# Products with zeros at twenty places of TensorE's program where it waits, in a hybrid RWKV-7 and mLSTM layer with a mixture of experts

## The chip, the cores and the metric

One core of a Trainium2 chip runs the whole layer in one launch. The metric is the device time of that launch in microseconds (us): the median of several runs. Engines are named TensorE (PE in the profile, with PEld for its weight loads), VectorE (DVE), ScalarE (ACT), GpSimd (POOL) and SyncE (SP, which here issues DMAs). TensorE multiplies a stationary operand, which is loaded first, with a moving operand of up to 512 columns, and writes into one of eight accumulation banks.

## The reference

The input x is 512 tokens of width 1024; 16 learned tokens are put ahead, so 528 are computed.

```
xn = rmsnorm(h);  proj = xn @ w_in          # r k v (512 each), q k (256 each), v o (512 each), gates
y_a = rwkv7(xn, r, k, v, ...)               # 8 heads of 64, per token:
      Sa = S a_t;  S = S * d_t + Sa b_t' + v_t k_t';  y_t = S r_t
      # the decay d and the rates a come from low-rank products with tanh and sigmoid; then a norm per head and a gate g
y_b = mlstm(q, k, v, o, gates)              # 4 heads, chunks of 64 tokens, matrix memory C, normaliser n, maximum m
h  = h + concat(y_a, y_b) @ w_out
xn = rmsnorm(h)
group = argmax over 4; the best 2 of its 8 experts, gate = pg * pe / sum(pe)
h  = h + sum over the two:  gate * ((silu(xn @ w_gate) * (xn @ w_up)) @ w_down)    # 32 experts, width 512
out = rmsnorm(h)[:, 16:]
```

## The kernel before

The serial recurrences are computed in chunks of 64 tokens. The RWKV heads go in four pairs j = 0..3 (two heads of 64 fill the 128 partitions). For each pair, `decays` (L788) makes decay and rate from 12 products of 64x264 (two times six), `norms` and `heads` the scaled vectors, `products` (L912) in two groups g of 32 products of 64x192 the triangular matrices inside all eight chunks, and at its end `p0`, those of the 16 learned tokens. `valued` (L890) brings v into place with four products into `pvt` and one into `pv0`. `inverse` (L1382) with `interleaved` (L1345) inverts the triangular matrices of all chunks and heads at once: VectorE does 31 serial steps, then TensorE joins the halves with 32x32 products (`pZ`, `pM`). `chain` (L1490) then goes through the chunks -1 to 7 one after the other: `removals` (L1432), `solved` (L1448), `next_state` (L1458), `outputs` (L1472). `gate_a` (L1313) makes the output gate in four accumulation groups of four products (`pgg`). The mLSTM half (`gates` L1133, `states` L1201, `outputs_b` L1259), the output projection with its residual (`mixer` L1866), and the experts follow. The experts run in 16 pairs in the loop at L2058: gate and up products at L2072, down products at L2130, weights fetched by DMA (L1740).

The projections of the input (`projections`, L1018) go in blocks given by the string PLAN (L34): 48 products of 128x264 in fp32r (8 steps k of 6), each block accumulating in two banks, or 24 of 128x512 for an `o` block. They are what TensorE does between the steps of the chain. The first blocks, before anything else can run, are computed in the loop at L632 to L648: for each k = 0..7, ScalarE and VectorE split the k-th slice of the input into a high and a low part, and `proj_k` (L600) multiplies with them.

The order of instructions on TensorE and SyncE is written by a planner, the class `Weave` (L359): each of the functions above is a generator with a rank, added in L1964 to L1983, and the planner goes on with the generator of the lowest rank whose time has come. `need` yields until a planned clock (class `Clock`, L181) says that the operands are written; `bank` yields until a bank is free. Every call through `P` (TensorE) or another engine's wrapper tells this clock what it costs (L300). The order on VectorE, ScalarE and GpSimd is left to the compiler's scheduler, which works with a simulated timeline (L2343). On the chip each engine runs its own program in order and waits at an instruction whose operands or whose bank are not ready.

At the start, nine products with zeros run before the first real one (L615 to L623):

```
    idle_ = A.get([128, 64], name="idle")
    V.memset(idle_, 0.0)
    pi = B.get(1, "idle", rest)
    for i in range(WARM):
        P.matmul(pi, idle_.bitcast(BF16), idle_.bitcast(BF16)[:, None].to_broadcast([128, 4, 128]), start=True, stop=True)
    B.put(pi)
    A.put(idle_)
```

Of the kernel before, what the change touches and what calls it, by code (L numbers as in the profile page):

```python
# [11 lines left out]
BF16 = mybir.dt.bfloat16  # L12
# [18 lines left out]
WARM = 9  # L31
FAR, EDGE = 0, 10
BLOCKS = "projected"
PLAN = "KLMRKRKVRVqRVvVvvqqqveaboooo"  # L34

CV = {}
# [322 lines left out]
class Weave:  # L359
# [4 lines left out]
    def __init__(self, clock, banks):  # L364
        self.clock, self.banks = clock, banks
        self.streams = []
        self.marks = set()
        self.spare = []
        self.n = self.rank = 0

    def add(self, rank, gen):
# [72 lines left out]
def layer(ctx, tc, a, out, dbg=None, stop=None):  # L444
# [169 lines left out]

    idle_ = A.get([128, 64], name="idle")  # L615
    V.memset(idle_, 0.0)
    pi = B.get(1, "idle", rest)
    for i in range(WARM):
        P.matmul(pi, idle_.bitcast(BF16), idle_.bitcast(BF16)[:, None].to_broadcast([128, 4, 128]), start=True, stop=True)
    B.put(pi)  # L620
    A.put(idle_)
    def squares(k):
        sq = A.get([128, L], name="sq") if k else acc  # L623
        if k % 2:
# [8 lines left out]
    for k in range(8):  # L633
        S.activation(xh[k], xT[:, k], AF.Copy, scale=c("nmw", k))
        V.scalar_tensor_tensor(xl[k], xT[:, k], c("nmw", k), xh[k].bitcast(F32), op0=OP.mult, op1=OP.subtract)
        proj_k(pk, kh_, kl_, k)
        if not k:
            first_block(2, 8)
            A.put(kraw)
        if k == 2:  # L640
            k1h, k1l, kput1 = split_block(stream.loaded.pop(0), hi_by=S, lo_by=V)
            for i in range(k):
                proj_k(pk1, k1h, k1l, i)
        if k >= 2:
            proj_k(pk1, k1h, k1l, k)
            squares(k - 2)
    for k in range(6, 8):
        squares(k)  # L648


    W = Weave(clock, B)
# [136 lines left out]
    def decays():  # L788

        yield from until("hwa")  # L790
        for j in range(4):
            if j > 1:
                yield from until(f"P{j - 2}")
            yield from W.units(A, 5)
            res = []
            js = slice(128 * j, 128 * j + 128)
            for i in range(2):
                yield from need(wah, wal, lbh, lbl)
                pg = yield from bank(2, "pg", rest)
                q = PAR[i]  # L800
                for n, (w, x) in enumerate(((lbh, wah), (lbh, wal), (lbl, wah))):
                    for h in range(2):
                        P.matmul(pg[:, h, :264], w[q, js], x[q, h * 264:h * 264 + 264], start=(n == 0),
                                 stop=(n == 2))
                t = A.get([128, L], name="sg" if i == 0 else "al")
                S.activation(halves(t), pg[:, :, :264], AF.Tanh, scale=0.5, bias=dv[:, 16 + 4 * i + j:17 + 4 * i + j])
                B.put(pg)
                G.tensor_scalar(t, t, 0.5, 0.5, op0=OP.mult, op1=OP.add)
                res.append(t)
                yield  # L810
            sg, al = res
            V.tensor_tensor_scan(sg, rst, sg, 0.0, OP.mult, OP.add)
            Dt = A.get([128, 537], name="Dt")
            D65 = Dt[:, 17:].rearrange("p (c t) -> p c t", t=65)
            G.memset(Dt[:, 0:1], 1.0)
            G.memset(D65[:, :, 0:1], 1.0)
            S.activation(Dt[:, 1:17], sg[:, :NM], AF.Exp, scale=-DEC)
            S.activation(D65[:, :, 1:], chunks(sg), AF.Exp, scale=-DEC)
            S.activation(sg, sg, AF.Exp, scale=DEC)
            gcopy(DT[:, j, 0:1], Dt[:, 16:17])  # L820
            gcopy(DT[:, j, 1:9], D65[:, :, 64])
            gates_of[j] = sg, al, Dt, D65
            W.mark(f"D{j}")
        A.put(wah, wal, lbh, lbl, rst)

    def norms():

        for j in range(4):
            yield from until(f"k{j}")
            yield from W.units(A, 1)  # L830
            sq = A.get([128, L], name="sq")
            S.activation(sq, kx[j], AF.Square, scale=c("k_k", j))
            yield from need(sq)
            pn = yield from bank(2, "pn", rest)
            for h in range(2):
                P.matmul(pn[:, h, :264], m("bones"), sq[:, h * 264:h * 264 + 264], start=True, stop=True)
            V.tensor_scalar(halves(sq), pn[:, :, :264], 1e-24, None, op0=OP.max)
            B.put(pn)
            S.activation(sq, sq, AF.Ln)
            S.activation(sq, sq, AF.Exp, scale=-0.5)  # L840
            V.scalar_tensor_tensor(sq, kx[j], c("k_k", j), sq, op0=OP.mult, op1=OP.mult)
            nks[j] = sq
            yield
            W.mark(f"n{j}")
# [45 lines left out]
    def valued(j, v):  # L890


        G.tensor_tensor(BV[:, j], BV[:, j], v[:, NM:], op=OP.mult)
        yield from need(v)
        pvt = yield from bank(1, "pvt", rest)
        for u in range(4):
            P.matmul(pvt[:, 128 * u:128 * u + 128], v[:, NM + 128 * u:NM + 128 * u + 128], cent, start=True, stop=True)
        pv0 = yield from bank(1, "pv0", rest)
        P.matmul(pv0[:NM, 0:128], v[:, :NM], cent, start=True, stop=True)
        for e in range(2):  # L900
            for p in range(2):
                q = PAR[1 - p]
                src = pvt[PAR[e]].rearrange("p (u x) -> p u x", u=4)[:, :, 64 * p:64 * p + 64]
                S.copy(Vs[q, e::2, j], src)
        S.copy(VU0[0:NM, j, 1], pv0[:NM, 64:128])
        S.copy(VU0[64:64 + NM, j, 0], pv0[:NM, 0:64])
        B.put(pvt, pv0)
        A.put(v)
        yield
        W.mark(f"V{j}")  # L910

    def products(j):  # L912

        for g in range(2):
            cs = slice(4 * g, 4 * g + 4)
            yield from need(Bbd, Kbd, MV)
            pB = yield from bank(2, "pAB", rest)
            pK = yield from bank(2, "pAK", rest)
            for i in range(4):
                xs = slice(192 * (i % 2), 192 * (i % 2) + 192)  # L920
                for pt, st, turn in ((pB, Bbd, 0), (pK, Kbd, 1)):
                    for p in range(2):
                        P.matmul(pt[PAR[p ^ turn], i // 2, xs], st[PAR[p], 4 * g + i], MV[PAR[p], 4 * g + i], start=True,
                                 stop=True)
# [22 lines left out]

        yield from need(K0bd, B0bd, mv0)
        p0 = yield from bank(1, "p0", rest)
        P.matmul(p0[:, 0:80], K0bd, mv0, start=True, stop=True)  # L950
        P.matmul(p0[:, 80:160], B0bd, mv0, start=True, stop=True)
        for p in range(2):
# [65 lines left out]
    def projections():  # L1018
# [3 lines left out]
        for i, kind in enumerate(PLAN):  # L1022
# [10 lines left out]
            for k in range(8):  # L1033
                if two:
                    proj_k(pt, hi, lo, k, cols=cols)
                else:
                    proj_k(pt.rearrange("p (a b) -> p a b", a=1), hi, lo, k, ((NM, T),))
                yield
                if k == 1 and i + 1 < len(PLAN):
                    if PLAN[i + 1] == "e":  # L1040
                        yield from until("lora")
                    ready = prepare(PLAN[i + 1])
                if k == 3:
                    stream.load()
# [268 lines left out]
    def gate_a():  # L1313
# [17 lines left out]
        for j in range(4):  # L1331
            js = slice(128 * j, 128 * j + 128)
            pgg = yield from bank(1, "pgg", every)
            for n, (u, v) in enumerate(((wh, xgh), (wh, xgl), (wl, xgh), (ws[0:96], xs[0:96]))):
                P.matmul(pgg, u[:, js], v, start=(n == 0), stop=(n == 3))
            S.activation(Gw[:, j], pgg, AF.Copy, scale=c("lnx_w", j))
            V.scalar_tensor_tensor(BV[:, j], BV[:, j], c("lnx_b", j), pgg, op0=OP.add, op1=OP.mult)
            B.put(pgg)
            yield
        yield from until("columns")  # L1340
        A.put(*held, hg, misc)
        W.mark("Gw")

# [38 lines left out]
    def inverse():  # L1382
# [12 lines left out]
        for uh in range(2):  # L1395
            yield from need(Y2)
            pZ = yield from bank(2, "pZ", rest)
            quarters = [(p, slice(64 * p, 64 * p + 32), slice(64 * p + 32, 64 * p + 64)) for p in range(2)]
            for u in range(16):
                for p, q0, q1 in quarters:  # L1400
# [10 lines left out]
        for uh in range(2):  # L1411
            us = slice(16 * uh, 16 * uh + 16)
            yield from need(Zs[uh], Y1)
            pM = yield from bank(2, "pM", rest)
            for u in range(16):
                for p, q0, q1 in quarters:
                    P.matmul(pM[q0, p, u * 32:u * 32 + 32], Zs[uh][q1, u], Y1[q1, :, 16 * uh + u], start=True,
# [72 lines left out]
    def chain():  # L1490
# [19 lines left out]
        for ch in range(-1, 8):  # L1510
            first = ch < 0
            vs, vu, nxt = (VU0, VU0, VS[0]) if first else (VS[ch % 2], VU[ch % 2], VS[(ch + 1) % 2])
            n = NM if first else 64
            yield from need(vs)
            removals(ch, first, vs, n)
            yield from need(Wt)
            solved(ch, first, vu, n)
            yield from need(vu)
            if ch < 7:
                next_state(ch, first, vu, nxt)  # L1520
                yield
# [825 lines left out]
```

## Time and profile before

| what | value |
|---|---|
| median of 3 runs | 904.93 us (900.92 to 907.99) |
| the profiled execution | 904.07 us |
| its span (first to last instruction on the engines) | 902.3 us |
| mean granted TensorE clock over the span | 0.958 of full speed |
| busy TensorE / VectorE / ScalarE / GpSimd | 826.9 / 434.1 / 264.3 / 203.1 us |

The profiled execution's own time is 1.8 us longer than its span. The busy times overlap. A granted clock of 1.00 is the 2.4 GHz level of TensorE, 0.50 the 1.2 GHz level. Matmuls are pipelined, so a TensorE that is busy all of a stretch is not always at its peak. Most instructions of the front part bear the line L308, since the wrapper that tells the planner issues them; they are told apart by tile, shape and time.

### The profile page before, as it was taken

What the parts mean: (1) busy time and instruction counts of PE and PEld (TensorE: products, weight loads), DVE (VectorE), ACT (ScalarE), POOL (GpSimd) and SP (SyncE); (2) the same over time, 40 slices, a digit from 0 to 9 for tenths busy, and PEclk for the clock granted to TensorE, in tenths of its full rate; (3) what the DMA queues carried; (4) which work ended last, traced back from release to release, by engine and by line L of the source; (5) the groups of instructions that cost most, each with busy time, mean ns of one, the idle gap of its engine ahead of it and who ended that gap; (6) DMA issues with size and microseconds to landing.
All of it is one profiled execution on the core that took longest, in us unless ns stands there. A gap on an engine that the chain in (4) does not pass through costs nothing. (4 is left out here: it accounts for less than half of the span.)

```text
span 902.3 us, 13658 instructions
## 1 busy us (share of the span) xinstructions
PE 826.9 (92%) x5487; PEld 499.0 (55%) x5488; DVE 434.1 (48%) x819; ACT 264.3 (29%) x505; POOL 203.1 (23%) x278
## 2 busy tenths in 40 slices
PE   7989697878899889999999999999999999999994
PEld 5878596777887767888343444433444423332331
DVE  7677757598746639437132333423333323331324
ACT  5755555634345584312110111001110101001102
POOL 5164625365543328220100000000000000000002
PEclk8988889988998899999999999999999999999998
DMA  6210111311300222989999999999999999999982
GB/s 238 71 42 7 47 63 55 83 34 38 102 25 2 74 84 72 386 329 348 376 406 393 419 420 420 420 420 420 420 420 420 420 421 420 420 419 422 421 349 97
DMA packets 45142, 235.60 MB, mean 261 GB/s; under 512 B 9906, under 2 KB 10290, under 8 KB 21008
## 3 DMA queue, kind: packets, MB, share of 16 engines
q1 hardware_dynamic: 42192, 228.58, 63.6%
q0 software_dynamic: 2160, 3.93, 1.1%
q10 hardware_dynamic: 720, 2.15, 0.6%
q8 instruction: 45, 0.74, 0.3%
q14 instruction: 25, 0.20, 0.1%
HBM read 234.38 MB, written 4.19 MB: 264 GB/s over the span
## 5 line engine op out<-in xcount | busy, mean ns | idle before, releaser
L308 PE MATMUL accs<-arS,arR 128*128 128x264 f32 (+2 forms) x1136 | 180.8, 311 | 8.3 <-DVE arS L308 3.5
L308 PEld LDWEIGHTS accs<-arS,arR 128*128 128x128 f32 (+1 forms) x1136 | 160.6, 199 | 22.4 <-issue 5.5
L308 PE MATMUL accs<-arF 64*64 64x192 f32 (+17 forms) x1361 | 112.6, 289 | 29.8 <-DVE arF L308 20.0
L2072 PE MATMUL accs<-arF 128*64 128x512 f32 x568 | 133.2, 599 | 6.2 <-DMA arF<-wgu 6.1
L2000 DVE TENSOR_TENSOR arF<-arF,accs 128x512 f32<-128x512 f32 x124 | 80.8, 683 | 100.4 <-PE accs L1998 98.9
L308 PEld LDWEIGHTS accs<-arF 64*64 64x64 f32 (+6 forms) x1346 | 83.1, 157 | 46.3 <-DVE arF L308 15.9
L308 POOL TENSOR_TENSOR arF<-arF 128x528 f32<-128x528 f32 (+13 forms) x97 | 89.9, 929 | 83.1 <-DVE arF L308 56.6
L1809 POOL DMA_INDIRECT arM<-hd,arF x15 | 15.1, 1008 | 372.8 <-DVE arF L1799 356.1
L308 DVE TENSOR_TENSOR arF<-arF 64x16 f32<-64x16 f32 (+31 forms) x170 | 90.2, 578 | 7.4 <-POOL arF L308 4.7
L2072 PEld LDWEIGHTS accs<-arF 128*64 128x64 f32 x568 | 37.5, 137 | 87.1 <-issue 65.3
L308 ACT ACTIVATE arF<-arF 128x528 f32<-128x528 f32 (+7 forms) x113 | 59.8, 550 | 74.7 <-DVE arF L308 51.5
L2107 ACT ACTIVATE arF<-accs,arF 128x512 f32<-128x512 f32 x16 | 11.0, 687 | 240.1 <-PE accs L2072 240.1
L308 POOL TENSOR_SCALAR arF<-arF 64x256 f32<-64x256 f32 (+9 forms) x101 | 56.9, 565 | 95.3 <-ACT arF L308 43.2
L2140 DVE SCALAR_TENSOR_TENSOR arO<-accs,arF,arO 128x1024 fp32r<-128x1024 f32 x15 | 19.3, 1284 | 103.2 <-ACT arO L2139 103.2
L2130 PE MATMUL accs<-arF 128*64 128x512 f32 x280 | 63.8, 597 | 0.2 <-DMA arF<-wdn 0.2
L1997 PE MATMUL accs<-arO,OHT 128*128 128x512 f32 x124 | 57.5, 464 | 0.0
L308 ACT COPY arF<-accs 64x256 f32<-64x256 f32 (+7 forms) x111 | 39.8, 370 | 53.8 <-PE accs L308 28.2
L308 DVE TENSOR_TENSOR arF<-accs,arF 128x128 f32<-128x128 f32 (+7 forms) x81 | 35.6, 460 | 29.0 <-PE accs L308 21.1
L1998 PE MATMUL accs<-arO,OHT 128*128 128x512 f32 x124 | 49.0, 395 | 0.0
L308 PE MATMUL accs<-arW,arS 128*128 128x512 f32 x192 | 46.7, 398 | 0.0
L1997 PEld LDWEIGHTS accs<-arO,OHT 128*128 128x128 f32 x124 | 23.3, 188 | 40.4 <-issue 38.1
L2139 ACT ACTIVATE arO<-accs,arF 128x1024 fp32r<-128x1024 f32 x15 | 16.7, 1113 | 98.7 <-PE accs L2130 98.7
(142 smaller groups left out, 930.3 us busy)
## 6 DMA issues: line engine op xcount, KB each, us to landing
arF<-wgu SPq DMA_DIRECT2D x71, 1024.0 KB, 19.8
arF<-wdn SPq DMA_DIRECT2D x35, 1024.0 KB, 19.8
arM<-wgu SPq DMA_DIRECT2D x23, 1024.0 KB, 20.0
arH<-wgu SPq DMA_DIRECT2D x17, 1024.0 KB, 19.8
arN<-wgu SPq DMA_DIRECT2D x16, 1024.0 KB, 18.6
arF<-wb SPq DMA_DIRECT2D x23, 512.0 KB, 3.6
arM<-wdn SPq DMA_DIRECT2D x10, 1024.0 KB, 20.5
arN<-wdn SPq DMA_DIRECT2D x8, 1024.0 KB, 20.4
```

Of the source, the lines that this page charges most:

```text
L308: r = f(*args, **kw)
L1809: nc.gpsimd.indirect_dma_start(out=xt[p % 2], out_offset=None, in_=hd, in_offset=bass.IndirectOffsetOnAxis(ap=idx[:, p % 2:p % 2 + 1], axi ...
L1997: P.matmul(pq, lhs, oh[:, hs], start=True, stop=False)
L1998: P.matmul(pq, lhs, ol[:, hs], start=False, stop=True)
L2000: V.tensor_tensor(hv, hv, pq, op=OP.add)
L2072: P.matmul(pgu[64 * e:64 * e + 64, h], x[:, k, 64 * e:64 * e + 64], w[:, D * e + 512 * h:D * e + 512 * h + 512], start=(k == 0), stop=(k = ...
L2107: S.activation(av, pgu[:, 0], AF.Silu, scale=r1_)
L2130: P.matmul(pdn[64 * e:64 * e + 64, h], aT[:, k, 64 * e:64 * e + 64], w[:, D * h + 512 * e:D * h + 512 * e + 512], start=(k == 0), stop=(k ...
L2139: S.activation(oh, pdf, AF.Copy, scale=g1_)
L2140: V.scalar_tensor_tensor(ol, pdf, g1_, oh.bitcast(F32), op0=OP.mult, op1=OP.subtract)
```

## The change

A table `HOLD` gives a number of products for each of twenty places. `keep(place)` issues that many products of the zero tile `idle_`, read as bf16: 128 stationary columns and a moving operand of 4 times 66, that is 264, columns (256 in `solved` of chunk 7). They are issued directly, not through the wrapper, so the planner's clock doesn't see them and the order of the other instructions on TensorE stays as it was. Where `to` names a bank that the next real products overwrite from their start, the zeros are written there first. Where it doesn't, they are added, as zeros, into the open accumulation of the projection block that is half done (`W.open`, which is set after each step k below 7). Places that have no entry issue nothing (`pn`, `pM`, `next` and other indices). The zero tile is kept until the end of `gate_a` and the bank `pi` until the end of the first loop. The counts add up to 255.

```diff
+HOLD = {("decays", 0, 0): 4, ("decays", 0, 1): 4, ("decays", 1, 0): 4, ("products", 0, 0): 19, ("products", 1, 0): 28,
+        ("decays", 3, 0): 11, ("decays", 3, 1): 20, ("p0", 2): 9, ("pvt", 1): 6, ("pv0", 1): 9, ("pvt", 2): 16,
+        ("pvt", 3): 28, ("pZ", 0): 22, ("solved", -1): 13, ("removals", 3): 9, ("solved", 7): 13, ("pgg", 0): 19,
+        ("first", 1): 8, ("first", 2): 8, ("first", 3): 5}
...
+        self.open = None
...
     V.memset(idle_, 0.0)
+    zeros = idle_.bitcast(BF16)
+
+    def keep(*site, to=None):
+
+        t = W.open if to is None else to
+        for _ in range(HOLD.get(site, 0) if t is not None else 0):
+            nc.tensor.matmul(t, zeros[:, :t.shape[0]], zeros[:, None, :t.shape[1] // 4].to_broadcast([128, 4, t.shape[1] // 4]),
+                             start=to is not None, stop=to is not None, skip_group_check=True)
+
     pi = B.get(1, "idle", rest)
...
-    B.put(pi)
-    A.put(idle_)
...
+        if k:
+            keep("first", k, to=pi[:, :264])
         proj_k(pk, kh_, kl_, k)
...
+    B.put(pi)                                    # after the first loop
...
                 pg = yield from bank(2, "pg", rest)
                 q = PAR[i]
+                keep("decays", j, i, to=None if j > 1 else pg[:, 0, :264])
...
+                keep("pn", j, h)
...
         pvt = yield from bank(1, "pvt", rest)
+        keep("pvt", j)
...
         pv0 = yield from bank(1, "pv0", rest)
+        keep("pv0", j)
...
             pB = yield from bank(2, "pAB", rest)
             pK = yield from bank(2, "pAK", rest)
+            keep("products", j, g, to=pB[:, 0, :264])
...
         p0 = yield from bank(1, "p0", rest)
+        keep("p0", j)
...
+                W.open = (pt[:cols, 0, :264] if two else pt[:cols, :264]) if k < 7 else None
                 yield
...
             pgg = yield from bank(1, "pgg", every)
+            keep("pgg", j, to=pgg[:, :264])
...
+        A.put(idle_)                             # end of gate_a
...
             pZ = yield from bank(2, "pZ", rest)
+            keep("pZ", uh)
...
             pM = yield from bank(2, "pM", rest)
+            keep("pM", uh)
...
             yield from need(vs)
+            keep("removals", ch)
             removals(ch, first, vs, n)
             yield from need(Wt)
+            keep("solved", ch, to=uv[:, 0].rearrange("p j x -> p (j x)") if ch > 6 else None)
             solved(ch, first, vu, n)
             yield from need(vu)
+            keep("next", ch)
```

## Rows read from the trace of the kernel before

**Rows 1.** The page: the span, the busy times of the engines with their share and number of instructions, and the granted clock of TensorE in 40 equal slices of the span, in tenths (9 is 90% or more).
```profile
span 902.3 us, 13658 instructions
PE 826.9 (92%) x5487; PEld 499.0 (55%) x5488; DVE 434.1 (48%) x819; ACT 264.3 (29%) x505; POOL 203.1 (23%) x278
PEclk8988889988998899999999999999999999999998
```

**Rows 2.** The view by stretches: begin and end in us from the span's start, length, then busy time and number of instructions of PE, PEld, DVE, ACT and POOL, the granted clock, the mean busy share of the DMA engines, GB/s. Just after the first zero products; from the end of the output gate to the last experts; inside the experts.
```profile
4.20:7.50 3.30, 1.83 (x8) 0.90 (x6) 1.62 (x10) 2.08 (x4) 0.00 (x0) 1.00 0.93 307
338.70:895.00 556.30, 537.60 (x2717) 245.37 (x2715) 202.89 (x411) 80.46 (x147) 51.49 (x58) 1.00 0.94 382
500.00:890.00 390.00, 379.18 (x1848) 144.05 (x1846) 124.75 (x220) 44.27 (x67) 12.99 (x17) 1.00 0.98 405
```

**Rows 3.** The same view, for the eleven stretches in which the granted clock is 0.50.
```profile
7.60:14.40 6.80, 4.22 (x17) 3.92 (x18) 6.77 (x6) 6.25 (x10) 4.31 (x3) 0.50 1.04 411
52.00:58.70 6.70, 6.48 (x29) 6.19 (x29) 4.67 (x6) 4.96 (x11) 6.20 (x8) 0.50 0.00 1
65.70:72.40 6.70, 6.11 (x40) 4.68 (x41) 5.39 (x10) 2.41 (x5) 1.30 (x5) 0.50 0.34 136
93.00:96.30 3.30, 2.68 (x32) 1.97 (x32) 3.30 (x4) 1.88 (x4) 2.74 (x3) 0.50 0.48 153
110.00:120.20 10.20, 6.99 (x27) 5.96 (x26) 8.23 (x11) 1.88 (x4) 4.01 (x6) 0.50 0.14 51
151.00:154.30 3.30, 3.30 (x15) 2.94 (x14) 2.35 (x5) 0.88 (x4) 1.03 (x5) 0.50 0.00 0
192.00:198.70 6.70, 5.51 (x23) 4.88 (x24) 6.63 (x17) 2.22 (x7) 4.21 (x10) 0.50 0.01 2
219.30:226.00 6.70, 6.70 (x135) 6.63 (x131) 2.70 (x3) 5.02 (x4) 5.04 (x4) 0.50 0.02 5
273.90:280.60 6.70, 6.70 (x64) 6.30 (x65) 2.12 (x5) 1.41 (x2) 0.30 (x1) 0.50 0.00 0
308.00:314.70 6.70, 6.51 (x45) 5.72 (x46) 3.72 (x9) 5.63 (x18) 1.44 (x2) 0.50 0.02 4
335.30:338.60 3.30, 3.30 (x9) 2.55 (x8) 1.78 (x3) 1.67 (x4) 1.84 (x1) 0.50 0.00 0
```

**Rows 4.** The timeline of TensorE: start in us, length in us, engine, line, operation, output and operands with their sizes, number of instructions in the row; in brackets the idle time before it and what ended it. Two groups of `products` (74.78 and 93.62) and the two halves of `decays` of pair 3.
```profile
74.78 1.53 PE L308 MATMUL accs<-arF 64*64 64x192 f32 x32
93.62 2.84 PE L308 MATMUL accs<-arF 64*64 64x192 f32 x32 [4.18 <-DVE arF L308]
108.22 0.99 PE L308 MATMUL accs<-arR 64*128 64x264 f32 x6 [1.83 <-ACT arF L308]
113.36 1.69 PE L308 MATMUL accs<-arR 64*128 64x264 f32 x6 [3.21 <-DVE arF L308]
```

**Rows 5.** The timeline of TensorE, same columns: the nine zero products at the start, and a block of the first projections.
```profile
1.02 3.66 PE L308 MATMUL accs<-arF 128*128 128x512 bf16 x9 [1.02 <-DVE arF L308]
29.68 5.64 PE L308 MATMUL accs<-arS,arQ 128*128 128x264 f32 x44 [0.50 <-DVE arQ L308]
```

**Rows 6.** The timeline of TensorE, same columns: `pv0` of pair 1, `removals` of chunk 3, `solved` of chunk 7, the first product of `pgg`.
```profile
150.87 0.57 PE L308 MATMUL accs<-arF 128*16 128x128 f32 x2 [1.42 <-DVE arF L308]
271.37 0.82 PE L308 MATMUL accs<-arF,arE 128*64 128x64 f32 x10 [1.43 <-DVE arF L308]
306.38 0.68 PE L308 MATMUL accs<-arF 64*64 64x64 f32 x16 [2.01 <-DVE arF L308]
334.00 0.49 PE L308 MATMUL accs<-arW 128*128 128x512 f32 x1 [2.92 <-ACT arW L308]
```

**Rows 7.** The timeline of ScalarE, same columns: copies of projections after `decays` of pair 3, and the activations that follow the chain's last chunk.
```profile
120.17 1.94 ACT L308 COPY arF<-accs 64x256 f32<-64x256 f32 x6 [3.45 <-PE accs L308]
315.35 0.34 ACT L308 ACTIVATE arF<-accs 128x4 f32<-128x4 f32 x2 [1.59 <-PE accs L308]
```

**Rows 8.** The view by stretches, columns as in rows 2: the inversion on VectorE, the stretch after the chain's last chunk, and the stretch after `gate_a`.
```profile
177.00:218.80 41.80, 33.10 (x243) 31.40 (x241) 41.08 (x111) 15.72 (x37) 24.60 (x44) 0.92 0.11 39
315.40:330.50 15.10, 15.10 (x82) 11.94 (x81) 4.44 (x10) 14.93 (x28) 2.02 (x2) 1.00 0.25 95
340.00:350.00 10.00, 10.00 (x45) 8.12 (x44) 9.12 (x7) 3.49 (x6) 9.57 (x7) 1.00 0.46 157
```

**Rows 9.** The timeline of TensorE, columns as in rows 4: `decays` of pair 1, the first products of pair 0 (two rows), projections before the inversion's end, `pZ`, and the projections after it.
```profile
52.27 1.69 PE L308 MATMUL accs<-arR 64*128 64x264 f32 x6 [0.22 <-ACT arF L308]
64.33 0.54 PE L308 MATMUL accs<-arF 64*64 64x192 f32 x2 [1.69 <-DVE arF L308]
66.29 3.51 PE L308 MATMUL accs<-arF 64*64 64x192 f32 x28 [1.43 <-DVE arF L308]
213.49 1.98 PE L308 MATMUL accs<-arS,arR 128*128 128x264 f32 x14 [0.73 <-POOL arR L308]
218.87 3.80 PE L308 MATMUL accs<-arF 32*32 32x32 f32 x128 [3.41 <-DVE arF L308]
222.61 4.71 PE L308 MATMUL accs<-arS,arR 128*128 128x264 f32 x24
```

**Rows 10.** The timeline of TensorE's weight loads, same columns: two of the loads of 128 columns in bf16 among the experts.
```profile
602.39 0.10 PEld L1794 LDWEIGHTS <-arF 128*128 128x128 bf16 x1 [0.81 <-issue]
602.43 0.10 PEld L1797 LDWEIGHTS <-arF 128*128 128x128 bf16 x1
```

## The prediction, made before the changed kernel ran

> **What bounds the kernel now.** I read the page's totals first: the span is 902.3 us, TensorE is busy 92% of it, and the line of its clock is at full speed only from the middle on; in the first 15 slices it drops eleven times or so [rows 1]. The profiled execution took 904.07 us, 1.8 more than its span, and 0.86 below the median of the runs shown (904.93). All sums below go against 904.07; the forecast for the median then adds 0.9.
>
> Then I read the views by stretch. From 338.7 us to 895 the clock is 1.00 and TensorE is busy 537.6 of 556.3 us; from 500 to 890 it is busy 379 of 390 us while the DMA engines are at 0.98 and 405 GB/s [rows 2]. Nothing of the change stands there. So this tail keeps its length and moves as a whole by what the front gains or loses. The front is where the change is, and there no engine is full all the time: it is a chain that goes from VectorE, ScalarE and GpSimd to TensorE and back, and each piece has to be judged by the wait that ends last in it.
>
> The third view is the list of stretches with a granted clock of 0.50, the 1.2 GHz level: eleven of them, 67 us together [rows 3]. For each I looked up what TensorE did before (it waited), and in the same stretch which engine was full. That price is visible in equal work: 32 products of 64x192 take 2.84 us in the stretch at 93 us, and 1.53 us at 74.78, where the clock was full [rows 4]. So TensorE's work at the low level costs nearly twice (2.84/1.53 = 1.86; the six 64x264 products give 1.69/0.99 = 1.71), and a stretch that is full of TensorE's work would end 0.41 to 0.46 of its length earlier at the high level.
>
> **What the change adds.** The counts of the twenty places add up to 255 products, nothing is removed, and the order of the real instructions on TensorE and SyncE stays. A product of zeros has 264 columns of bf16. The nearest rows: nine bf16 products of 512 columns at the start take 3.66 us, 0.407 each, so about 0.21 for 264 columns; 44 products of 264 columns in fp32r, at a full clock, take 5.64 us, 0.128 each [rows 5]. The start's nine ran at the pace that is half of what they would at the high level (0.407 for 512 columns against 0.128 for 264 is 1.6 times per column), so 264 bf16 columns lie between 0.105 (half of 0.21) and 0.128 at the high level, and at 0.21 at the low one. I take 0.11 while the clock is high.
>
> At 0.11 each, 28 products are 3.1 us of the 4.18 us wait before the second group of products of head pair 0; 11 and 20 are 1.2 and 2.2 of the 1.83 and 3.21 us before `decays` of pair 3 [rows 4]; 9 are 1.0 of 1.42 (`pv0`); 9 are 1.0 of 1.43 (`removals` of chunk 3); 13 are 1.4 of 2.01 (`solved` of chunk 7); 19 are 2.1 of 2.92 (`pgg`) [rows 6]. The zeros wait for nothing that is late, so they run inside the wait and end 0.3 to 1.1 us ahead of the real work. Their own cost is nothing at this price; the cover is gone at 0.15 us each (4.18/28).
>
> **Where a full clock would pay**, with the stage's own last wait:
> - 93.0 to 96.3: the 32 products themselves, 2.84 to 1.53, with VectorE waiting for their result: 1.3 us.
> - 113.4 to 120.2: TensorE is busy without a gap [rows 3], and ScalarE's copies at 120.17 had waited 3.45 us for it [rows 7]. 6.8 us times 0.41 to 0.46 is 2.8 to 3.1: 3.0.
> - 151.0 to 154.3: full of TensorE's work (3.30 of 3.30); 1.4 to 1.5: 1.5.
> - 273.9 to 280.6: full too (6.70 of 6.70), the chain of chunks, in which the other engines are idle [rows 3]: 3.0.
> - 308.0 to 314.7: TensorE would save 3.0, but ScalarE, in order, had waited only 1.59 us for it before 315.35, and is then busy 14.93 of 15.1 us [rows 7, 8]. What is late next is ScalarE: 1.5.
> - 335.3 to 338.6: TensorE would save 1.4, but from 340 to 350 GpSimd is busy 9.57 and VectorE 9.12 of 10 us [rows 8]. Bounds 0 and 1.2: 0.6.
>
> **Where it would pay nothing.**
> - 7.6 to 14.4: VectorE is busy 6.77 of 6.80 us [rows 3]; the early products follow its splits.
> - 52.0 to 58.7: GpSimd is busy 6.20 of 6.70 us, VectorE follows it, and TensorE waits for VectorE until 64.33 [rows 3, 9]. `decays` of pair 1 gets four zeros ahead of it in the same bank; bounds 0 and 0.5, I charge 0.25.
> - 65.7 to 72.4: bounds 0 and 1.4. TensorE's waits of 1.69 and 1.43 us get 19 zeros, 2.1 us [rows 9]. But if the stretch at 52 is at a full clock, TensorE arrives there some 3 us earlier and waits longer, beyond what the zeros fill. I take 0.
> - 192.0 to 198.7: VectorE inverts the triangular matrices in 31 serial steps, busy 41.08 of 41.80 us from 177 to 218.8 [rows 8]. TensorE there has time. 0.
> - 219.3 to 226.0: 24 projection products at the low level (4.71 us), 14 earlier ones at the high take 1.98, so 24 would be 3.4; bounds 0 and 1.3 [rows 9]. TensorE will reach the wait before 213.49 (0.73 us, for GpSimd) about 3 us earlier, and no zeros stand there; I expect the clock to fall in that longer wait, the 22 zeros then cost 0.21 each, 4.6 us against a wait of 3.41. 0, and down to -1.2.
>
> Sum: 1.3 + 3.0 + 1.5 + 3.0 + 1.5 + 0.6 - 0.25 = 10.65 us. 904.07 - 10.65 = 893.4; on the scale of the median, 894. Upper end of the gain: with 1.4, 1.3, and 0.6 more, and 1.5 more at 308 if ScalarE's order is helped too, some 15 us, 889. A further 4 us if stretches I do not count shorten VectorE's waits: 885.
>
> **The rivals.**
> *A: the falls move.* When TensorE is faster in one stretch, it arrives earlier at its next wait, which is then longer than in the trace the counts can be compared with, and the clock falls there. For it: the wait that ends right at the fall at 52 is of 0.22 us alone [rows 9], and the zeros leave a quarter to a third of each wait open. Against it: the big waits are filled. If only 93, 113 and 151 pay fully (5.8 us) and the rest is lost again: 904.93 - 5.5 = 899.
> *B, slower: the zeros are late.* If a zero product costs 0.21 us, each place on the chain runs over its wait: 28 x 0.21 - 4.18 = 1.7, then 1.0 (20), 1.2 (22), 1.1 (19), 0.7 (13), 0.5 (9), 0.5 (9), 0.5 (11), 0.9 (the first 19): 8.1 us on 150 products, and about 2 on the smaller places. It decides from 0.15 us each. If the clock stays as it is, that is 904.93 + 10 = 915. Against it: at the start TensorE ran nothing but nine zero products, and from 4.2 on its clock was 1.00 [rows 2, 5].
> *C: the loads come in series.* Each zero product loads its 128 columns again. A bf16 load of 128x128 is busy 0.10 us [rows 10]; added to 0.11 that is 0.21 us, now with a full clock: the 10 us of rival B cancel the 10.65 us gained, 904.
>
> On this the Trainium skill ("TensorE: Matmul & The Clock Gate", "LDWEIGHTS (loading the stationary operand)") puts a load in ns at its number of columns over 1.2, 107 ns for 128, and the page's section "The mechanism" lets a load overlap only products in other row groups, which the zeros are not. By that rule the sum would be rival C's. The trace disagrees on the overlap: two such loads of full height start at 602.39 and 602.43, with 0.10 us each, so they are not paid one after the other [rows 10].
>
> *D: it does something else.* The order on VectorE, ScalarE and GpSimd is left to the scheduler, which sees 255 instructions more; 64 words of on-chip memory and one bank are held longer. A changed order costs or brings a few us by chance: 904, 3 either way.
>
> **How the numbers follow.** Forecast 894: 0.53. A, 899: 0.25. B, 915: 0.07. C, 904: 0.05. D, 904: 0.10. One per cent, 9 us, is about what a measurement of this kernel can tell from no change: under 895.9 is faster, over 914 slower. The forecast's own spread (the halves taken at 65, 219, 308, 335) is 887 to 898 and lies mostly under 895.9; nearly all of A and D is within 1%. So faster 0.52, same 0.40, slower 0.08. The range for 8 in 10 takes in the forecast, its upper bounds, A, and most of C and D: 885 to 905.
>
> **What would show it.** Right: granted clock about 1.00 where rows 3 have 0.50, at 93, 113, 151, 274 and 308 above all; the 32 products at 93 in 1.5 us; groups of 28, 20 and 22 bf16 products at 0.11 us each; the inversion by VectorE starting some 5 us earlier, still 41 us long; the tail unchanged in length. New low stretches likely at about 66 and 213. Wrong: zero products at 0.2 us in a full clock (B, C); as many low stretches as before at other places (A); a tail that takes longer, since the front's gain would then be given back at the experts' loads.

## The result: 0.7% slower

The changed kernel took 909.39 us in the median of 14 runs (905.31 to 912.74), the kernel before 902.66 on the same chip (14 runs): ratio 1.0071, 95% interval 1.0054 to 1.0087, some 6.4 us slower by the ratio. The forecast was 894, with 885 to 905 as its range. Ratios below are each against runs of the kernel before on the same chip; the interval stands in brackets.

The page after, answering [rows 1]: the clock is higher (mean 0.976 against 0.958), 255 products more, and the span is 3.6 us longer.
```profile
span 905.9 us, 14165 instructions
PE 843.6 (93%) x5742; PEld 512.4 (57%) x5743; DVE 430.0 (47%) x819; ACT 265.1 (29%) x505; POOL 204.2 (23%) x278
PEclk9998999998899999999999999999999999999997
```

Six stretches of [rows 3] in the changed kernel, among its new low ones, then the tail of [rows 2] (columns as there):
```profile
52.00:58.70 6.70, 6.70 (x57) 6.16 (x56) 5.01 (x7) 5.24 (x11) 6.08 (x7) 1.00 0.02 4
93.00:96.30 3.30, 2.27 (x29) 1.81 (x30) 2.06 (x4) 2.79 (x6) 0.61 (x2) 1.00 0.00 0
110.00:120.20 10.20, 9.23 (x69) 8.00 (x69) 8.93 (x12) 5.83 (x11) 6.52 (x8) 1.00 0.08 9
151.00:154.30 3.30, 3.30 (x30) 3.30 (x29) 3.25 (x7) 1.79 (x2) 0.11 (x1) 1.00 0.01 2
192.00:198.70 6.70, 5.79 (x48) 5.56 (x48) 6.63 (x19) 3.37 (x10) 5.83 (x15) 1.00 0.23 78
210.70:217.50 6.80, 3.33 (x15) 3.23 (x16) 3.83 (x6) 1.33 (x1) 5.29 (x7) 0.50 0.00 1
224.40:227.70 3.30, 3.30 (x17) 3.30 (x17) 0.98 (x2) 0.88 (x2) 0.31 (x1) 0.50 0.64 209
231.20:234.50 3.30, 3.30 (x47) 3.23 (x42) 1.40 (x2) 2.00 (x4) 0.80 (x2) 0.50 0.36 81
275.60:278.90 3.30, 3.30 (x28) 3.16 (x28) 0.72 (x3) 0.36 (x1) 0.00 (x0) 0.50 0.02 5
308.00:314.70 6.70, 6.35 (x86) 5.19 (x85) 4.68 (x11) 5.97 (x18) 1.88 (x2) 1.00 0.23 71
320.00:323.30 3.30, 2.98 (x13) 2.96 (x14) 0.50 (x2) 3.24 (x7) 0.00 (x0) 0.50 0.00 0
391.60:395.00 3.40, 3.40 (x12) 2.90 (x11) 0.00 (x0) 0.00 (x0) 0.00 (x0) 0.50 1.01 422
500.00:890.00 390.00, 380.21 (x1866) 145.05 (x1862) 125.64 (x221) 43.10 (x61) 11.74 (x13) 1.00 0.99 410
```
The zeros do to the clock what was forecast: 52, 93, 110, 151, 192 and 308 stand at 1.00, and the new fall at 210.7 is where it was expected. Up to 890 us eight low stretches are left, 34 us together (two are not shown, at 12.7 and 67.3), where there were eleven and 67 us; those at 231.2, 320.0 and 391.6 were not foreseen.

TensorE's timeline after (columns as in rows 4), from five stretches:
```profile
91.75 2.97 PE L629 MATMUL accs<-arF 128*128 128x264 bf16 x25
95.76 1.53 PE L313 MATMUL accs<-arF 64*64 64x192 f32 x32 [1.03 <-DVE arF L313]
...
110.82 2.42 PE L629 MATMUL accs<-arF 128*128 128x264 bf16 x20
114.21 0.99 PE L313 MATMUL accs<-arR 64*128 64x264 f32 x6 [0.97 <-DVE arF L313]
...
214.16 3.45 PE L313 MATMUL accs<-arS,arR 128*128 128x264 f32 x14 [7.13 <-POOL arR L313]
217.41 2.70 PE L629 MATMUL accs<-arF 128*128 128x264 bf16 x22
220.04 3.17 PE L313 MATMUL accs<-arF 32*32 32x32 f32 x106
...
306.82 1.58 PE L629 MATMUL accs<-arF 128*128 128x256 bf16 x13 [2.16 <-DVE arF L313]
...
320.32 1.33 PE L313 MATMUL accs<-arS,arR 128*128 128x264 f32 x4 [2.51 <-DVE arF L313]
...
329.27 1.89 PE L313 MATMUL accs<-arS,arR 128*128 128x512 f32 x7 [1.42 <-DVE arF L313]
```
Set beside [rows 4, 6, 9], the same instructions show where time came and went. "Ahead" and "behind" below compare the start of the same instruction in two profiled executions, one of each kernel. At 114.21 TensorE is 0.85 us later than before (113.36), and 6 products take 0.99 in place of 1.69; by 194 it is 6 us ahead. VectorE's inversion, too, ends 6 us earlier, at 211.3. Then the lead is lost: 14 projections wait 7.13 us for GpSimd (0.73 before) and begin at 214.16, 0.7 us later than before; `pZ`, 218.87 before, begins at 220.04. `solved` of chunk 7 follows its zeros at 308.33 (306.38 before), and two waits that were not there (2.51 and 1.42 us) bring TensorE 4.6 us behind at 329. By 339 it has 3.0 of these back (1.6 behind), since it has neither the wait of 2.92 us nor the low stretch that the kernel before has there [rows 3, 6]; a wait at 387 that is 0.6 longer and the new fall at 391.6 take 2.2 again.

Why GpSimd was late, in its timeline after:
```profile
210.60 0.95 POOL L313 TENSOR_SCALAR arF<-arF 64x256 f32<-64x256 f32 x2 [5.71 <-DVE arF L313]
211.50 0.30 POOL L313 MEMSET arF<- 128x256 f32 x1
211.77 2.34 POOL L313 TENSOR_TENSOR arR<-arF,arR 128x1024 fp32r<-128x1024 f32 x1
```
The last row is the split of a projection block, for which TensorE waits. Before, it ran straight after the 128x64 row and ahead of the two copies and the memset; now these, which prepare the chain and wait for the inversion's last steps, stand first, and the engine works in order. ScalarE's timeline after shows a change of order too:
```profile
315.51 0.31 ACT L313 ACTIVATE arF<-accs 128x128 f32<-128x128 f32 x1
315.67 0.25 ACT L313 ACTIVATION_READ_ACCUMULATOR arF<-accs 128x1 f32 x1
315.94 1.28 ACT L313 ACT_TABLE_LOAD   x1
317.23 0.69 ACT L313 ACTIVATE arF<-accs,arF 128x512 f32<-128x512 f32 x1
317.82 0.27 ACT L313 ACTIVATE arF<-accs 128x128 f32<-128x128 f32 x1
...
327.05 0.27 ACT L313 ACTIVATE arF<-accs 128x128 f32<-128x128 f32 x1
```
Sums of squares over 128 columns stand between table loads, as before; but the last one now comes at 327.05, behind three table loads, and VectorE's next step waits for it until 327.44. Before, it came at 321.24, ahead of three table loads that now stand before it:
```profile
321.24 0.26 ACT L308 ACTIVATE arF<-accs 128x128 f32<-128x128 f32 x1
321.60 1.28 ACT L308 ACT_TABLE_LOAD   x1
```

### The profile page after: what moved, and what is told of

The parts are those of the page before. It is cut to its first block, busy times and chain, and to the rows that moved or that the text cites. A ratio compares the mean times of both kernels' runs of the same rounds, so it can differ in the third digit from the quotient of the medians.

```text
span 905.9 us, 14165 instructions
## 1 busy us (share of the span) xinstructions
PE 843.6 (93%) x5742; PEld 512.4 (57%) x5743; DVE 430.0 (47%) x819; ACT 265.1 (29%) x505; POOL 204.2 (23%) x278
## 5 line engine op out<-in xcount | busy, mean ns | idle before, releaser
L313 PE MATMUL accs<-arS,arR 128*128 128x264 f32 (+2 forms) x1136 | 178.6, 309 | 17.2 <-POOL arR L313 7.1
L313 PEld LDWEIGHTS accs<-arS,arR 128*128 128x128 f32 (+1 forms) x1136 | 158.6, 196 | 30.2 <-POOL arR L313 7.3
L313 PE MATMUL accs<-arF 64*64 64x192 f32 (+17 forms) x1361 | 105.4, 276 | 14.7 <-DVE arF L313 9.7
L313 PEld LDWEIGHTS accs<-arF 64*64 64x64 f32 (+6 forms) x1346 | 77.1, 146 | 30.0 <-DVE arF L313 9.2
L313 DVE TENSOR_TENSOR arF<-arF 64x16 f32<-64x16 f32 (+31 forms) x170 | 86.6, 556 | 11.7 <-POOL arF L313 4.6
L313 DVE SCALAR_TENSOR_TENSOR arF<-arF 128x528 f32<-128x528 f32 (+5 forms) x50 | 32.8, 663 | 28.7 <-ACT arF L313 27.7
```

The costliest lines, as they stand in the source:

```text
L313: r = f(*args, **kw)
```

## The experiments

The first theory: the scheduler, once it sees the zeros, orders GpSimd, ScalarE and VectorE otherwise, and that costs more than the clock brings. Rivals: the zero tile, held longer, moves the other buffers; or the zeros themselves are late on TensorE.

| run | median us | ratio to before |
|---|---|---|
| changed kernel | 909.4 | 1.0071 [1.0054, 1.0087] |
| e1 held tile, no zeros | 908.2 | 1.0056 [1.0036, 1.0077] |
| e2 split first | 912.3 | 1.0097 [1.0061, 1.0133] |
| e3 no pvt(3) | 909.0 | 1.0064 [1.0038, 1.0089] |
| e4 no solved(7) | 910.0 | 1.0076 [1.0053, 1.0099] |
| e5 own tile, no zeros | 904.2 | 0.9992 [0.9977, 1.0006] |
| e6 own tile, zeros | 914.1 | 1.0112 [1.0088, 1.0135] |
| e7 zeros, order pinned | 898.7 | 0.9939 [0.9919, 0.9959] |
| e8 ten places, pinned | 896.5 | 0.9908 [0.9886, 0.9931] |
| e9 order of e1 alone | 915.2 | 1.0127 [1.0105, 1.0148] |
| e10 order of the changed kernel alone | 922.1 | 1.0203 [1.0178, 1.0228] |
| e11 e7 without solved(7) | 898.1 | 0.9934 [0.9911, 0.9957] |
| e12 three places, pinned | 901.1 | 0.9966 [0.9946, 0.9987] |
| e13 e7, GpSimd's order free | 902.5 | 0.9988 [0.9969, 1.0006] |
| e14 e7, ScalarE's order free | 907.4 | 1.0030 [1.0009, 1.0051] |
| e15 e7, GpSimd's and VectorE's free | 921.4 | 1.0189 [1.0160, 1.0219] |

(e8 leaves out ten of the twenty places and keeps ten, with 143 products; its label and its expectation miscount them.)

**e1**
```diff
-HOLD = {("decays", 0, 0): 4, ...
+HOLD = {}
```


> The changed kernel with an empty table: no zero product is issued, only the zero tile and its bank are held longer. Theory (the order of GpSimd and ScalarE, set by the scheduler once it sees the zeros, costs the time): within 2 us of the kernel before, eleven stretches at a granted clock of 0.50 as there. Rival (the tile held longer moves the other buffers and that alone costs): 5 to 7 us slower than the kernel before.

The rival came true, against the theory: no zero product, the low stretches of before up to 316, and 5 us lost. The built program has the order of before on TensorE and GpSimd, a changed one on VectorE and ScalarE after 300, and one expert weight DMA of SyncE later in its queue. In its profile TensorE is 5.6 us behind at 328, where the last sum of squares comes late as in the changed kernel, but 0.4 behind at 339; a longer wait at 386 (0.6) and a new fall at 390.8 to 394.2 (1.6) make it 2.9 again. So most of what its profile loses in the end (3.4 us of span) is lost there, without any zeros.

**e2**
```diff
+        gate = splits[-2]          # the split of a projection block on GpSimd
+        with tc.issue_after(gate):
             G.memset(Wt, 0.0)
...
+        with tc.issue_after(gate):
             values(0)
```
(and the same around values(1); `splits` lists GpSimd's splits as they are issued)

> The changed kernel with all its zeros and the same order on TensorE and ScalarE; on GpSimd alone the copies and the memset that prepare the chain are ordered behind the split of a projection block. Theory (these copies wait for the end of the inversion and hold up the split, for which TensorE waits 7.13 us): that wait falls under 2 us, the first pZ product comes 4 to 6 us earlier, and the whole is 4 to 5 us faster than the changed kernel, about 905. Rival (the zeros themselves are late on TensorE, the wait is a symptom): the wait is replaced by another one of the same size, 909 as before.

Half a miss. The 7.13 us wait is gone (3.27 us are left at 204), and `pZ` begins at 216.26 instead of 220.04. But TensorE then waits 2.39 us for ScalarE at `solved` of chunk -1, where the changed kernel waits 0.30, and the whole is not faster: of the 3.8 us 1.6 are left there and 0.2 at 300, and at 400, after falls at 353.8 to 357.2 and 391.4 to 398.2, TensorE is 2.1 us behind the changed kernel. The place was mended and the loss moved on.

**e3, e4**
```diff
-        ("pvt", 3): 28,                      # e3
-        ("solved", 7): 13,                   # e4
```


> The changed kernel without the 28 zero products before pvt of pair 3; built so, GpSimd's order around the inversion's end is that of the kernel before. Theory: a low stretch at about 190 comes back, which costs nothing since VectorE's inversion is the bound there, and the 7.13 us wait goes: 3 to 5 us faster than the changed kernel, 904 to 906. Rival (a full clock at that place is worth something): 909 or slower.

> The changed kernel without the 13 zero products before solved of chunk 7. Theory (these zeros are written into the bank that VectorE is still reading, so they start only when the real products could, and with them ScalarE's order after the chain changed): the wait of 2.16 us before a zero product at 304.7 is gone, solved of chunk 7 comes 1.5 to 2 us earlier, the stretch to 330 another 2 us: 2 to 4 us faster, 905 to 907. Rival (they hold the clock for the chain's last stretch): a low stretch comes back at 308 and the time is 909 or more.

Both missed in the total. In e3 the 7 us wait is gone (1.35 us are left), and TensorE is still ahead of before at 232; the waits at 303, 318 and 329 bring it 5.5 us behind (4.6 in the changed kernel). e4 went as its rival said: `solved` of chunk 7 came no earlier (308.74), and the low stretch came back, at 310 to 317. So neither place alone was the cause, and e1 had shown one that has no zeros in it.

**e5, e6**
```diff
-    zeros = idle_.bitcast(BF16)
+    zt = sb.tile([128, 8], F32, name="zt")
+    nc.gpsimd.memset(zt, 0.0)
+    zeros = zt.bitcast(BF16)         # read with a step of 0 as 128 stationary and 264 moving columns
...
+    B.put(pi)                        # both back where they were
+    A.put(idle_)
-            keep("first", k, to=pi[:, :264])
```
(e5 with an empty HOLD, e6 with the rest of it)

> No zero products; the tile for them is eight words outside the memory that the other buffers share, and the first zero tile and its bank go back where the kernel before puts them back. Theory (holding the 64 words and the bank is what cost 5 us in e1, because it moved other buffers and with them the order on ScalarE and VectorE): the program is the kernel before with one memset more, so its time too, within 2 us. Rival (e1 was slow by chance of the build): 907 or more.

> The zeros of all places but the three of the first loop (234 products), from the tile of e5; the order on VectorE, ScalarE and GpSimd is left to the scheduler. Theory (two costs, the held tile and the orders that the zeros bring about): the part of the held tile is gone, 5 us less than the changed kernel, about 904; the 7 us wait before 214 and late weights or statistics remain where the order differs. Rival (only the held tile costs): all gains of the clock show, 894 to 898.

e5 is the kernel before, in its order on every engine and in its time: what e1 lost came with the held tile. e6 missed on the worse side: without the held tile, but with the orders that 234 zeros bring about, 914.

**e7, e8**
```diff
+    for e, runs in ORDER.items():    # V, S, G: the order in which the kernel before has its instructions
+        ins, line = LOG[e], [t for a0, a1 in runs for t in range(a0, a1)]
+        for i, j in zip(line, line[1:]):
+            tc.add_manual_dep(ins[j], ins[i].name, mybir.DependencyInfo(mybir.DependencyClass.NoSync, mybir.DependencyReason.DATA), reason="order")
```


> As e6, with the order of every instruction on VectorE, ScalarE and GpSimd up to the experts pinned to that of the kernel before; TensorE and SyncE have theirs already. Theory (the zeros do to the clock what the prediction said, and the orders gave it back): few low stretches, TensorE 6 us ahead at 211 and after it, 894 to 898. Rival (zeros on the path cost what the clock gives): 902 to 906.

> As e7, without the zeros at decays of pairs 0 and 1, pvt of pairs 2 and 3, pZ and solved of chunk 7: eleven places, 143 products, those in whose stretch TensorE sets the end or whose zeros wait for no reader of a bank. Theory (these other places cost or bring nothing): as fast as e7 or 1 to 3 us faster, since the 2 to 3 us lost before 67 and the 2 us at solved of chunk 7 are gone: 892 to 897. Rival (low stretches come back at 52, 192 and 219 and count): 2 to 4 us slower than e7.

The decisive pair. e7 has e6's zeros, memory and TensorE program, and only the order on three engines is another: 898.7 in place of 914.1. In the traces e7 has, leaving out the zeros, the order of e5 instruction by instruction, and e5 takes the time of the kernel before; so the order that is pinned brings nothing by itself. e8 has the lowest median: 0.92% under the kernel before, 8.3 us (6.2 to 10.3), though its six runs overlap with those of e7. Both beat both kernels.

**e9, e10** (the program of e5, ORDER taken from e1 and from the changed kernel)

> No zero products and no held tile: the program of e5, with VectorE, ScalarE and GpSimd pinned to the order that they have in e1. Theory (the held tile costs through the order alone): 4 to 6 us slower than the kernel before, 908, with ScalarE's reductions after 315 split by an activation of 512 columns as in e1. Rival (the moved buffers, or the one moved DMA on SyncE, cost in e1): as the kernel before.

> No zero products and no held tile: the program of e5, with VectorE, ScalarE and GpSimd pinned to the order of the changed kernel. Theory (orders cost what the clock brought): the changed kernel without its gains, 914 to 919, with a wait of TensorE for the weights' split before 214. Rival (that order is good only or bad only together with the zeros): 902 to 908.

The orders alone, without a zero or a moved buffer, cost 11.5 and 18.4 us (1.27 and 2.03% of 904). Both lost more than expected (908; 914 to 919). e9 lost more than e1, which has the same order on VectorE, ScalarE and GpSimd: in e9 ScalarE, in order, waits for a weight that had come in time in e1, and so it does in e10 (first e9, then e10):
```profile
318.67 0.62 ACT L316 CAST arW<-arF 128x512 fp32r<-128x512 f32 x1 [5.58 <-DMA arF<-wo]
```
```profile
325.65 0.62 ACT L316 CAST arW<-arF 128x512 fp32r<-128x512 f32 x1 [9.00 <-DMA arF<-wo]
```
In the changed kernel no wait of ScalarE for these weights is longer than 1.1 us. TensorE loses 10.0 us in e9 and 10.7 in e10 between the instructions that the kernel before has at 312 and at 325; e1 and the changed kernel lose 4.8 and 4.3 there. So 11.5 and 18.4 are not what these orders cost in the kernels that they come from; e10 does show the wait for the split (6.21 us before 218.04).

**e11, e12** (pinned; HOLD without solved(7); HOLD with products(1,0), decays(3,0), decays(3,1) alone)

> As e7, without the 13 zero products before solved of chunk 7, which waited 2.09 us for the bank that VectorE was reading and ran behind that wait. Theory (those zeros alone cost 1.5 to 2.3 us there): 896 to 897, solved of chunk 7 at 301.2 to 301.5 instead of 303.4. Rival (without them a low stretch at 308 takes back as much): 898 to 899.

> Order pinned to that of the kernel before; zeros at three places alone: products of pair 1 (28), decays of pair 3 (11 and 20). By the terms of the prediction these bring 1.3 and 3.0 us: 4 us faster than the kernel before, 900, with TensorE 4 us ahead from 121 on. Rival (the gain is given back at the inversion, where VectorE sets the pace, or at the next unfilled wait): 903 to 905.

e11: the theory of those thirteen zeros fell. They do run behind the bank's reader, but without them the clock is at 0.50 from 303 to 310, and the time is the same. e12: 3.1 us (1.2 to 4.9) where 4.3 were expected. In its profile TensorE is 2.2 us behind before 93 and 2.3 ahead at 121, so that the two places bring 4.4.

**e13, e14, e15** (e7 with some engines' ORDER taken from e6)

> As e7 (zeros, pinned order), but GpSimd has the order that it has in e6; VectorE and ScalarE keep that of the kernel before. Theory (copies ahead of the split hold up TensorE by 7 us, and behind it pZ and the chain): TensorE waits 6 to 7 us before the projections at 213, 4 to 6 us slower than e7, 903 to 905. Rival (GpSimd's order is a symptom, the loss of e6 lies with ScalarE): as e7, 899.

> As e7, but ScalarE has the order that it has in e6. Theory (ScalarE's order holds up the chain at 282 to 284 and 308, where TensorE waits 2.45 and 3.3 us in e6): 5 to 8 us slower than e7, 904 to 907, nearly all of it after 280. Rival (GpSimd's order alone makes the loss): as e7, 899.

> As e7, but GpSimd and VectorE have the order that they have in e6. Theory (VectorE's order adds little to GpSimd's, since it waits for the others): 0 to 3 us slower than e13. Rival (VectorE's order is the main loss): 910 or more, as e6.

GpSimd's order alone costs about 4 us against e7, ScalarE's alone about 8: the first at the wait that was named, the second at the two that were named and, 4 us in its profile, at a fall at 353.0 to 359.8 that was not. GpSimd, first e7, then e13, and TensorE's wait in e13:
```profile
205.16 0.65 POOL L316 TENSOR_SCALAR arF<-arF 128x64 f32<-128x64 f32 x1 [5.92 <-DVE arF L316]
205.79 2.34 POOL L316 TENSOR_TENSOR arR<-arF,arR 128x1024 fp32r<-128x1024 f32 x1
```
```profile
208.94 0.95 POOL L316 TENSOR_SCALAR arF<-arF 64x256 f32<-64x256 f32 x2 [3.42 <-DVE arF L316]
209.84 0.30 POOL L316 MEMSET arF<- 128x256 f32 x1
210.12 2.34 POOL L316 TENSOR_TENSOR arR<-arF,arR 128x1024 fp32r<-128x1024 f32 x1
```
```profile
212.50 3.45 PE L316 MATMUL accs<-arS,arR 128*128 128x264 f32 x14 [7.14 <-POOL arR L316]
```
ScalarE, first e7, then e14: four activations ahead of the chain's copy, and twelve. TensorE, in e14, waits 2.45 us for that copy.
```profile
278.81 1.28 ACT L316 ACTIVATE arF<-arF 128x128 f32<-128x128 f32 x4 [0.75 <-DVE arF L316]
279.99 0.35 ACT L316 COPY arF<-accs 64x256 f32<-64x256 f32 x1
```
```profile
279.56 3.61 ACT L316 ACTIVATE arF<-arF 128x128 f32<-128x128 f32 x12 [1.17 <-DVE arF L316]
283.08 0.35 ACT L316 COPY arF<-accs 64x256 f32<-64x256 f32 x1
```
e15 missed: with VectorE's order too it is 19 us slower than e13, and slower than e6, in which all three are free. TensorE falls behind e7 by 3.5 us at 65, 8 at 216 and 23 at 760. The largest piece, 11 us, is lost from 283 to 326, where TensorE waits 2.80, 3.25 and 2.21 us for VectorE (in e7 once, 2.09) and the clock is at 0.50 from 292.9 to 299.8 and from 313.4 to 327.1; why VectorE is late there stays open. The orders of the engines fit each other, and their costs don't add.

## Why the prediction was wrong

The step that failed is the order of the other engines. The sum has no term for it: its sentence on what the change adds says only that the order on TensorE and SyncE stays (on SyncE one DMA moved). Rival D alone has it, and prices it too low: "A changed order costs or brings a few us by chance: 904, 3 either way", with a chance of 0.10. With the same zeros, the same memory and the same program of TensorE and SyncE, the orders that the scheduler made cost 15.4 us against those of the kernel before (e6, 914.1; e7, 898.7). Even the change without zeros costs 5 (e1); rival D names the held words and the bank, but within the same 3 us. The range ended at 905, since it held nothing of that size. For the changed kernel itself the cause is shown in part: its wait of 7.13 us comes with GpSimd's order alone (7.14 in e13), and what it loses by 325 comes without zeros too (e1); a run of it with the old order is missing.

The rest of the sum, point by point, with the pinned runs beside the changed kernel. Each figure of TensorE's place is of one execution, and those differ: up to 45 us e7, e13 and e14 have the same instructions in the same order, and e13 alone falls to 0.50 there, from 30.7 to 34.2, which takes 1.5 us.
- Price of a zero product: 0.11 expected; 25 in 2.97 and 20 in 2.42 us are 0.12. So the prices of rivals B and C did not come; with the clock mostly at 0.50 a zero product took 0.185 (22 in 4.07 us before `pZ` in e7). By the Trainium skill ("TensorE: Matmul & The Clock Gate", "LDWEIGHTS (loading the stationary operand)") a load of 128 columns takes 107 ns; in series with the product that makes 0.22 us, an estimate, and the trace does not have it.
- 93: 1.3 expected; 1.53 us in place of 2.84, as said. 113: 3.0 expected; in the changed kernel TensorE is 0.85 us late when the second half of `decays` of pair 3 runs at 114.21 and 2.3 ahead at 118, 3.1. Together 4.4, and 4.4 by TensorE's place in e12 too; e12's time is 3.1 us less (1.2 to 4.9), which doesn't contradict it.
- 151: 1.5 expected, 1.3 in the changed kernel and in e7; but e12, which has no zeros there, gains the same 1.3.
- 52 and the waits at 64: -0.25 expected. In the changed kernel the first products of pair 0 came 1.3 us late (65.67 against 64.33), in e7 0.7 early (63.67). Why is not shown: in e5, which has no zeros, they came 1.2 early, and e6, whose order is free, is as late as e7 at 80 (0.7 and 0.6 us).
- 213 and 219: the fall at a longer wait before the projections came as expected (low from 210.7 to 217.5); the wait was 7.13 us and not some 4, since GpSimd's row was late. Pinned, it is 2.76 (e7), with the low stretch at 209.7 to 213.1.
- 274: 3.0 expected; half of the low stretch stayed (275.6 to 278.9), and TensorE gains 0.9 there, 1.3 in e7. This term was too large: the zeros before chunk 3 did not hold the clock through the next chunks. In e8, with the same zeros, the clock was at 0.50 from 269.1 to 275.9 and nothing was gained.
- 308: 1.5 expected; in e7 nothing. I had not seen that these zeros write into a bank that VectorE still reads: they wait as long as the real products did, and run behind that wait. TensorE is 5.3 us ahead before them, 3.0 after them, and 4.8 at the end of the stretch: the clock gives back what the zeros cost. e11, without them, takes the same time.
- 335: 0.6 expected, between 0 and 1.2; 1.6 in e7 (4.8 to 6.3 ahead).
- The sum: 10.65 expected; 5.5 (3.7 to 7.3) with all places but the first loop's, 8.3 (6.2 to 10.3) with the ten of e8.
- The tail was to move whole. It nearly did; but a fall at 391.6 to 395.0 in the changed kernel, and at 381.8 to 388.5 in e8, took 1.6 and 3.1 us of TensorE's place that no step had foreseen. e1 loses 1.6 in the same way without a zero product, e7 nothing.
- A reading: the page's line of the clock [rows 1] is under 9 in nine of its first 15 slices, not eleven; eleven is the number of stretches in [rows 3].

Rival A, the falls move, is what the pinned runs show. It had 93, 113 and 151 paying 5.8 us and the rest lost again: in e7 TensorE gains 5.9 from 93 to 155 (0.6 behind to 5.3 ahead) and is 4.8 ahead at 318, and the kernel takes 898.7 where rival A said 899 (in part by luck: the 1.6 at 335 are not in rival A's sum). Not tried: the order of the kernel before on the changed kernel itself; its moved buffers make other instructions wait for each other, and the old order may not fit them. Open is how much of e1's 5 us is order, how much the moved buffers and the one DMA that SyncE issues later, and how much the fall at 391; e9 can't tell, since e1's order, on other buffers, cost more there than in e1.

## What to carry to other kernels

Where some engines' orders come from a scheduler with costs, an edit to another engine's program, or to what memory is held, is an edit to all of them: price it first with the edit made empty (e1), then pin the order to that of the kernel before (e7), and only then judge the idea. An order is fitted to its buffers and to the other engines' orders, so mending it at one place (e2) moved the loss. Work put into a wait must itself wait for nothing: a bank that is about to be overwritten may still be read.

## What had not been expected of the hardware

- TensorE busy without a gap at a low clock: in e8, with 6.70 of 6.70 us busy, nearly all on products of 512 columns, it stayed at 0.50 from 381.8 to 388.5. In e7 the same instructions, behind the same wait of 0.44 us, ran at 1.00: the 27 products of 512 columns took 9.18 us in e8 and 6.50 in e7. So the same work of TensorE ran at either level.
```profile
381.80:388.50 6.70, 6.70 (x20) 5.44 (x20) 0.00 (x0) 0.00 (x0) 0.00 (x0) 0.50 1.01 421
```
- Four operations of the inversion on VectorE took 3.32 us before, while GpSimd's split ran (from 211.06, 2.38 us), and the same four 0.92 us after, where the split ran later. That is 2.4 of the 6 us by which the inversion ended earlier, and it comes from the split's place and not from the clock: e7 and e13, which differ in GpSimd's order alone, show it. One operation of the inversion takes 2.31 us in e7, where the split runs beside it (from 205.79), and 0.29 in e13, where the split runs later (from 210.12); the inversion ends at 212.2 and 209.6. The Trainium skill ("SBUF — State Buffer", "Terms") says that these two engines take turns at one pair of ports, held for a whole instruction; the numbers agree with it. Before, changed kernel, e7, e13:
```profile
210.69 3.32 DVE L308 TENSOR_TENSOR arF<-arF 128x84 f32<-128x84 f32 x4
```
```profile
207.05 0.92 DVE L313 TENSOR_TENSOR arF<-arF 128x84 f32<-128x84 f32 x4
```
```profile
205.96 2.31 DVE L316 TENSOR_TENSOR arF<-arF 128x78 f32<-128x78 f32 x1
```
```profile
205.82 0.29 DVE L316 TENSOR_TENSOR arF<-arF 128x78 f32<-128x78 f32 x1
```
